# Two accumulation groups side by side in two PSUM banks, in a two-layer streaming encoder

## The chip, the cores and the metric

The kernel runs on one core of one Trainium2 chip. The metric is the device time of one execution in microseconds (us). Three executions of the kernel before took 1283.43, 1287.02 and 1288.18 us; the median is 1287.02.

Engines are named as the profile names them: PE is TensorE (matmuls), PEld its loading of weights, DVE is VectorE, ACT is ScalarE, POOL is GpSimd, SP is SyncE, which here issues the DMAs. PSUM, into which matmuls accumulate, has eight banks of 512 float32 columns in each of 128 partitions.

## The reference

The input x is (1, 512, 1024) float32. There are two layers. The first mixes by stick-breaking attention, the second by forgetting attention; both end with a gated feed-forward layer. Norms before and after each part are left out here.

```python
# layer 0: 16 heads of 64
q, k, v = split(a @ sb_w_qkv, 3)
h = h + rmsnorm(stick_breaking(q, k, v) @ sb_w_o)
# layer 1: softmax over s <= t of q.k/8 + fcum[t] - fcum[s]
kvf = rmsnorm(h) @ w_kvf            # keys, values, 16 forget gates
q = rmsnorm(h) @ fox_w_q
h = h + rmsnorm(forgetting(q, k, v, fcum) @ fox_w_o)
# at the end of each layer, d_ff = 2816
hdn = causal_conv_width_3(rmsnorm(h) @ w_up) + conv_b
gate, up = split(hdn, 2)
h = h + rmsnorm((gelu(gate) * up) @ w_down)
```

## The kernel before

**Matmuls in three passes.** Each float32 operand is kept as two exact parts, a high and a low one, and each product is made of three matmuls: high by high, high by low, low by high. The normalized activations are held feature-major as AH and AL, eight slices of 128 features by 512 tokens. A product over 1024 features is thus a group of 24 matmuls that accumulate into one PSUM region.

**Weights.** A stream of tiles of 512 KB is loaded in a fixed order by SP into two raw buffers. `make` (L127) splits each into its two parts, in ScalarE (L142, or L136 with a gain) and VectorE (L146, or L137). A ring of NW = 8 pairs of buffers holds them. `take` (L157) hands out the next tile and asks for the one eight places further on, which reuses the buffers of the tile handed out.

**Products with the weights stationary.** `w_stationary` (L205) runs the 24 matmuls (L211) of one group into one bank, 512 tokens wide, or 256 when it is called by halves. The feed-forward layer calls it through `up` (L574) for the gate and then for the up part of one chunk of 128 features, into the two banks of a pair; four pairs take turns over the 22 chunks. `gate` (L578) then applies the convolution (L585, L587), the GELU (L592) and the product (L593). The first three chunks (EARLY) are run by halves of the tokens, since the later token blocks come later. `gates` (L291) uses the function for the forget gates.

**Projections of the attention.** `project` (L345 and on) makes the query and the key of one pair of heads: it takes the query's tile, runs its group into one bank and reads this out (L357 and, in layer 1, L359 on ScalarE, L360 on VectorE, for each half of the partitions); then it takes the key's tile, runs its group into the other bank and reads that out (L369, L370 on ScalarE, L371 on VectorE). `project_v` makes the values of two pairs of heads: for each of the four token blocks it runs 24 matmuls of 256 columns (L389), two blocks to a bank, and reads a bank out (L394, L395). Both functions get their banks from `bank("pj")`, banks 4 and 5 in turn, except at the start of an attention, where banks that are not yet otherwise in use are passed in.

**Heads.** `head` (L400 and on) makes one head's scores (L409) in banks 0 to 2, its weights on ScalarE and VectorE, transposes them on TensorE (L456) into banks 6 and 7 and multiplies them with the values (L468) in bank 3.

**Order.** `run` writes, for each pair p: head (p, 0), the projection of pair p + 1, head (p, 1) and, for every second pair, the values of the next two. The framework's scheduler lays down each engine's order when the program is built, from this order of writing and from when it expects an instruction's inputs and buffers; semaphores are set by it, in PSUM by bank. So matmuls of a projection and of heads stand mixed on TensorE.

**Token-major products.** `unit` (L504) does the two products that follow, with the activations stationary and two banks in turn (L511). In the last block of the last layer `down_proj` runs it for one bank at a time.

Of the kernel before, what the change touches and what calls it, by code (L numbers as in the profile page):

```python
# [14 lines left out]
P = 128  # L15
T = 512
D = 1024
# [15 lines left out]
# Column offset of each query block's row of scores, and its width.  # L33
# [9 lines left out]
def tile_trunk(  # L43
# [29 lines left out]
    # All of PSUM, by banks. Attention: scores 0-2, weighted values 3, projections 4-5, transposes 6-7.  # L73
    # Elsewhere: pairs of banks, one for each token block or chunk of features in flight.
# [15 lines left out]
    # mask_a keeps keys before the query, mask_b those up to it.  # L90
# [10 lines left out]
    # Residual stream by token blocks; normalized activations, feature-major, in two parts.  # L101
# [9 lines left out]
    # Row p stands for head p % 16 and is of kind p % 64 // 16: kinds 0, 2 or 3, 1; less 2, 0 or 1, less 3.  # L111
# [3 lines left out]
    # ---- weight stream: each tile arrives whole and is split into two exact parts. Pool takes few of them:  # L115
    # it and DVE's operations on two operands in SBUF exclude each other. ----
# [88 lines left out]
    def w_stationary(ps, w, t0=0, t1=T, m=P):  # L205
        hi, lo = w
        n = 3 * KT
        i = 0
        for k in range(KT):
            for a, b in ((hi, AH), (hi, AL), (lo, AH)):  # L210
                nc.tensor.matmul(ps, a[:, k, :m], b[:, k, t0:t1], start=i == 0, stop=i == n - 1)  # L211
                i += 1

# [1 line left out]
    def rstd_of(ss):  # L215
        """(sum / D + eps) ** -0.5 of ss's first column, into its column 3."""
        nc.gpsimd.tensor_scalar(ss[:, 2:3], ss[:, 0:1], 1.0 / D, EPS, op0=ALU.mult, op1=ALU.add)  # L217
        nc.gpsimd.tensor_tensor(out=ss[:, 3:4], in0=ss[:, 2:3], in1=mhalf, op=ALU.pow)
        return ss[:, 3:4]

    def pre_block(b, g, t4, junk):
        """Normalizes block b of the residual and puts it into AH and AL."""
# [14 lines left out]
    def post_block(b, y, g, t4, junk):  # L237
        """Adds the normalized y to block b of the residual."""
        ss = small.tile([P, 4], F32, name="ss")
        nc.scalar.activation(junk, y, AF.Square, accum_out=ss[:, 0:1])  # L240
        nc.vector.tensor_tensor(out=t4, in0=y, in1=g, op=ALU.mult)
        r = rstd_of(ss)
        nc.vector.scalar_tensor_tensor(
            out=H[:, b, :], in0=t4, scalar=r, in1=H[:, b, :], op0=ALU.mult, op1=ALU.add
        )

    def finish(b, y, g, t4, junk):
        """post_block for the last block, by halves, with its way out."""
# [22 lines left out]
    class Attn:  # L271
# [19 lines left out]
        def gates(self):  # L291
            """Running sums of the log forget gates, and what adds fcum[t] - fcum[s] to a head's scores:
            rows (fcum in two parts, 1, 1) by query times rows (1, 1, -fcum in two parts) by key, the rows
            of all heads, 16 to a kind, in both halves of the partitions."""
# [14 lines left out]
            for t0 in (0, T // 2):  # L309
                w_stationary(ps[:, t0 : t0 + T // 2], ws, t0, t0 + T // 2)  # L310
# [27 lines left out]
        def gate_keys(self, p):  # L338
            """The rows by key of pair p's heads."""
# [5 lines left out]
        def project(self, p, halves=1, banks=None):  # L345
# [4 lines left out]
            w = take()  # L350
            ps = PS[:, banks[0], :] if banks else bank("pj")
            n = T // halves
            for j in range(halves):
                w_stationary(ps[:, j * n : (j + 1) * n], w, j * n, (j + 1) * n)
# [9 lines left out]
            w = take()  # L364
            ps = PS[:, banks[1], :] if banks else bank("pj")
            for j in range(halves):
                w_stationary(ps[:, j * n : (j + 1) * n], w, j * n, (j + 1) * n)
# [8 lines left out]
        def project_v(self, g, banks=None):  # L376
# [3 lines left out]
            for b0 in range(0, NB, per):  # L380
                ps = PS[:, banks[b0], :256] if banks else bank("pj")
                for b in range(b0, b0 + per):
                    sl = slice(b * P, (b + 1) * P)
                    o = slice((b - b0) * 256, (b - b0 + 1) * 256)
                    i = 0
                    for k in range(KT):
                        hi, lo = (w0, w1)[k // 4]
                        for a, m in ((AH, hi), (AH, lo), (AL, hi)):
                            nc.tensor.matmul(ps[:, o], a[:, k, sl], m[:, k % 4, :], start=i == 0, stop=i == 3 * KT - 1)  # L389
                            i += 1  # L390
# [9 lines left out]
        def head(self, p, hh):  # L400
# [38 lines left out]
            else:  # L439
                # exp(z), guarded where sigmoid(z) is 1 and its complement under float32's rounding.  # L440
# [79 lines left out]
    def out_proj(done, heads_end):  # L520
        """Block by block, around the last head's transposes and products."""
# [38 lines left out]
    def ffn_phase(l, heads_end, post_g, next_g, final):  # L560
        with tc.tile_pool(name=f"ffn{l}", bufs=2) as pool:
# [12 lines left out]
            def up(c, w, t0, t1):  # L574
                for i in range(2):
                    w_stationary(pair_of(c)[:, i, t0:t1], w[i], t0, t1)
# [132 lines left out]
```

## Time and profile before

| what | value |
|---|---|
| runs | 1283.43, 1287.02, 1288.18 us |
| profiled execution, span from the first to the last instruction | 1282.6 us; no other time of it is shown |
| instructions | 16820 |
| PE busy | 1241.5 us (97%) in 6485 matmuls |
| PEld busy | 1054.6 us (82%) |
| DVE busy | 811.0 us (63%) |
| ACT busy | 644.4 us (50%) |
| POOL busy | 101.8 us (8%) |
| DMA | 111.97 MB, 87 GB/s |
| mean granted TensorE clock | 0.996 of full speed |

The busy time of PE counts each matmul to its modelled end, and successive matmuls overlap, so the pace of matmuls is to be read from their starts or from their number in a stretch. The heads of the first attention run until about 247 us, its product with the output weights and the feed-forward layer until about 648 us, the second attention until about 850 us, and the rest is the second feed-forward layer. In a timeline the columns are start, duration, engine, line, operation, output and inputs, shape and count; in square brackets stands how long the engine was idle before, and what ended that. In the chain a row is start, duration and what the time was spent on.

### The profile page before, as it was taken

To read this page: it belongs to the slowest core of one execution; us is meant where nothing else is said; L and a number is where in the kernel's file an instruction comes from. 1 tells how busy PE (TensorE), PEld (TensorE's weight loads), DVE (VectorE), ACT (ScalarE), POOL (GpSimd) and SP (SyncE) were. 2 spreads that over 40 slices of the span, in tenths; PEclk is the share of its full clock that TensorE was granted. 3 is DMA by queue.
4 is the path that set the end of the run, shared out by engine and by line. 5 is a ranking of instruction groups with operands and counts; after the bars stand their busy time and mean duration, and the time that the engine had idled before them with its cause. 6 is when DMAs were issued, how large, how long until landed. Compare 5 with 4: busy or idle time off the path is not lost.

```text
span 1282.6 us, 16820 instructions
## 1 busy us (share of the span) xinstructions
PE 1241.5 (97%) x6485; PEld 1054.6 (82%) x6485; DVE 811.0 (63%) x1304; ACT 644.4 (50%) x1085; POOL 101.8 (8%) x163
## 2 busy tenths in 40 slices
PE   6999998999999999999989999999999999999998
PEld 6888886789888888888888988978988888888886
DVE  6898899576655555433478887874685555554323
ACT  5767677454433333322488786674453333333221
POOL 1000003020000000000011212342100000000001
PEclk9999999999999999999999999999999999999999
DMA  6421212124333333333223122110543233323311
GB/s 214 138 66 50 67 50 66 33 86 144 101 97 99 92 90 99 88 109 90 75 68 99 51 82 67 50 51 33 148 132 98 84 97 99 94 87 98 99 33 66
DMA packets 145928, 111.97 MB, mean 87 GB/s; under 512 B 4680, under 2 KB 136120, under 8 KB 145848
## 3 DMA queue, kind: packets, MB, share of 16 engines
q1 hardware_dynamic: 145848, 110.90, 28.8%
q8 instruction: 51, 0.84, 0.3%
q14 instruction: 29, 0.24, 0.1%
HBM read 108.79 MB, written 2.10 MB: 86 GB/s over the span
## 4 chain that ended last, share of the span: by engine, by line
PE 77%; DVE 10%; ACT 5%; DMA 4%; issue 2%; POOL 0%; SPq 0%; DVEq 0%; POOLq 0%; ACTq 0%
PE PS L211 45%; PE PS L511 21%; PE PS L389 4%; PE PS L468 2%; PE PS L409 2%; DVE wlo L146 2%; DMA raw<-sb_w_qkv_dram 2%; DVE ec L446 2%; PE PS L456 2%; DMA raw<-w_up_dram 2%; DVE ec L448 1%; DVE PL L463 1%; ACT whi L142 1%; ACT whi L136 1%; ACT ec L445 1%
## 5 line engine op out<-in xcount | busy, mean ns | idle before, releaser
L211 PE MATMUL PS<-AH,whi 128*128 128x512 f32 (+1 forms) x1088 | 402.0, 370 | 5.5 <-DVE QS L360 3.8
L211 PE MATMUL PS<-AL,whi 128*128 128x512 f32 (+1 forms) x1088 | 401.2, 369 | 0.0
L211 PE MATMUL PS<-AH,wlo 128*128 128x512 f32 (+1 forms) x1088 | 401.0, 369 | 0.0
L146 DVE TENSOR_TENSOR wlo<-raw,whi 128x512 fp32r<-128x512 f32 x332 | 217.4, 697 | 224.5 <-ACT whi L142 223.7
L142 ACT CAST whi<-raw 128x1024 fp32r<-128x1024 f32 x172 | 180.4, 1049 | 237.9 <-PE PS L211 186.4
L211 PEld LDWEIGHTS PS<-AH,whi 128*128 128x128 f32 x1088 | 204.8, 188 | 43.5 <-DVE QS L360 4.9
L211 PEld LDWEIGHTS PS<-AH,wlo 128*128 128x128 f32 x1088 | 204.5, 188 | 36.7
L211 PEld LDWEIGHTS PS<-AL,whi 128*128 128x128 f32 x1088 | 204.8, 188 | 36.2
L587 DVE SCALAR_TENSOR_TENSOR hc<-PS,cw,hc 128x511 f32<-128x511 f32 (+1 forms) x176 | 130.7, 746 | 2.7
L511 PE MATMUL PS<-whi,al 128*128 128x512 f32 x352 | 109.5, 389 | 0.0
L511 PE MATMUL PS<-whi,ah 128*128 128x512 f32 x352 | 109.3, 389 | 0.0
L511 PE MATMUL PS<-wlo,ah 128*128 128x512 f32 x352 | 109.3, 389 | 0.0
L610 DVE TENSOR_TENSOR al<-act,ah 128x512 fp32r<-128x512 f32 x44 | 30.4, 690 | 117.4 <-ACT ah L609 117.4
L609 ACT CAST ah<-act 128x512 fp32r<-128x512 f32 x44 | 27.4, 622 | 144.7 <-PE PS L511 138.5
L217 POOL TENSOR_SCALAR ss<-ss 128x1 f32<-128x1 f32 x31 | 11.7, 376 | 830.9 <-ACT junk L240 764.8
L389 PE MATMUL PS<-whi,AH 128*128 128x256 f32 x256 | 74.1, 289 | 3.5 <-DVE AL L235 1.4
L511 PEld LDWEIGHTS PS<-whi,ah 128*128 128x128 f32 x352 | 66.1, 188 | 13.7
L511 PEld LDWEIGHTS PS<-whi,al 128*128 128x128 f32 x352 | 66.1, 188 | 13.7
L511 PEld LDWEIGHTS PS<-wlo,ah 128*128 128x128 f32 x352 | 66.1, 188 | 13.7
L389 PE MATMUL PS<-wlo,AH 128*128 128x256 f32 x256 | 74.0, 289 | 0.0
L389 PE MATMUL PS<-whi,AL 128*128 128x256 f32 x256 | 73.5, 287 | 0.0
L592 ACT ACTIVATE hc<-hc 128x512 f32<-128x512 f32 x44 | 27.8, 631 | 86.3 <-DVE hc L587 86.3
(130 smaller groups left out, 1758.9 us busy)
## 6 DMA issues: line engine op xcount, KB each, us to landing
raw<-w_up_dram SPq DMA_DIRECT2D x88, 512.0 KB
raw<-w_down_dram SPq DMA_DIRECT2D x44, 512.0 KB
raw<-sb_w_qkv_dram SPq DMA_DIRECT2D x24, 512.0 KB
raw<-w_kvf_dram SPq DMA_DIRECT2D x16, 512.0 KB
raw<-sb_w_o_dram SPq DMA_DIRECT2D x8, 512.0 KB
raw<-fox_w_q_dram SPq DMA_DIRECT2D x8, 512.0 KB
raw<-fox_w_o_dram SPq DMA_DIRECT2D x8, 512.0 KB
H<-x_dram SPq DMA_DIRECT2D x4, 512.0 KB
```

Source lines behind the costliest of these rows:

```text
L142: nc.scalar.copy(hi, raw)
L146: eng.tensor_tensor(out=fl[:, s], in0=fr[:, s], in1=fh[:, s], op=ALU.subtract)
L211: nc.tensor.matmul(ps, a[:, k, :m], b[:, k, t0:t1], start=i == 0, stop=i == n - 1)
L389: nc.tensor.matmul(ps[:, o], a[:, k, sl], m[:, k % 4, :], start=i == 0, stop=i == 3 * KT - 1)
L409: nc.tensor.matmul(z[:, ZOFF[b] : ZOFF[b] + n], a[:, b * P : (b + 1) * P], m[:, :n], start=i == 0, stop=i == len(passes) - 1,)
L446: nc.vector.tensor_tensor_scan(C[:, ::-1], self.R[:, ::-1], C[:, ::-1], 0.0, ALU.mult, ALU.add)
L456: tr = nc.tensor.transpose(zt[:, o : o + P], E[:, ZOFF[b] + j * P : ZOFF[b] + (j + 1) * P], ident)
L511: mm = nc.tensor.matmul(y[:, c, :], s[:, sl], m[:, 0, c * 512 : (c + 1) * 512], start=k == 0 and i == 0, stop=k == n - 1 and i == 2,)
L587: nc.vector.scalar_tensor_tensor(out=hc[:, s:], in0=y[:, i, : T - s], scalar=col[:, 2 - s : 3 - s], in1=hc[:, s:], op0=ALU.mult, op1=ALU.add,)
L592: uses_table(nc.scalar.activation(hs[0], hs[0], AF.Gelu_apprx_tanh))
L609: nc.scalar.copy(ah, act[:, k, :])
L610: nc.vector.tensor_tensor(out=al, in0=act[:, k, :], in1=f32(ah), op=ALU.subtract)
```

## The change

`w_stationary` gets lists: several outputs and as many weight tiles. For each slice and each pass it runs one matmul for each of them before it goes on, so that two groups of 24 become one sequence of 48 that alternates between two banks. `up` passes gate and up of a chunk together. `project` takes both tiles first, runs query and key together, then reads out the query's bank and after it the key's. `project_v`, where it uses banks 4 and 5, takes both banks first and runs blocks 0 and 2 side by side, then blocks 1 and 3, and reads both banks out after that; with four banks passed in it runs block after block as before and reads them all out afterwards. `gates` passes lists of one.

```diff
-    def w_stationary(ps, w, t0=0, t1=T, m=P):
-        hi, lo = w
+    def w_stationary(outs, ws, t0=0, t1=T, m=P):
         n = 3 * KT
         i = 0
         for k in range(KT):
-            for a, b in ((hi, AH), (hi, AL), (lo, AH)):
-                nc.tensor.matmul(ps, a[:, k, :m], b[:, k, t0:t1], start=i == 0, stop=i == n - 1)
+            for a, b in ((0, AH), (0, AL), (1, AH)):
+                for ps, w in zip(outs, ws):
+                    nc.tensor.matmul(ps, w[a][:, k, :m], b[:, k, t0:t1], start=i == 0, stop=i == n - 1)
                 i += 1
...
-            w = take()
-            ps = PS[:, banks[0], :] if banks else bank("pj")
+            ws = [take(), take()]
+            pq, pk = (PS[:, b, :] for b in banks) if banks else (bank("pj"), bank("pj"))
             n = T // halves
             for j in range(halves):
-                w_stationary(ps[:, j * n : (j + 1) * n], w, j * n, (j + 1) * n)
+                w_stationary([x[:, j * n : (j + 1) * n] for x in (pq, pk)], ws, j * n, (j + 1) * n)
+            ps = pq
...
-            w = take()
-            ps = PS[:, banks[1], :] if banks else bank("pj")
-            for j in range(halves):
-                w_stationary(ps[:, j * n : (j + 1) * n], w, j * n, (j + 1) * n)
+            ps = pk
...
-            for b0 in range(0, NB, per):
-                ps = PS[:, banks[b0], :256] if banks else bank("pj")
-                for b in range(b0, b0 + per):
-                    sl = slice(b * P, (b + 1) * P)
-                    o = slice((b - b0) * 256, (b - b0 + 1) * 256)
-                    i = 0
-                    for k in range(KT):
-                        hi, lo = (w0, w1)[k // 4]
-                        for a, m in ((AH, hi), (AH, lo), (AL, hi)):
-                            nc.tensor.matmul(ps[:, o], a[:, k, sl], m[:, k % 4, :], start=i == 0, stop=i == 3 * KT - 1)
-                            i += 1
+            if banks:
+                pss = {b: PS[:, banks[b], :256] for b in range(NB)}
+                groups = [(b,) for b in range(NB)]
+            else:
+                pss = {0: bank("pj"), 2: bank("pj")}
+                groups = [(0, 2), (1, 3)]
+            for grp in groups:
+                i = 0
+                for k in range(KT):
+                    hi, lo = (w0, w1)[k // 4]
+                    for a, m in ((AH, hi), (AH, lo), (AL, hi)):
+                        for b in grp:
+                            b0 = b // per * per
+                            nc.tensor.matmul(
+                                pss[b0][:, (b - b0) * 256 : (b - b0 + 1) * 256],
+                                a[:, k, b * P : (b + 1) * P], m[:, k % 4, :], start=i == 0, stop=i == 3 * KT - 1,
+                            )
+                        i += 1
+            for b0, ps in pss.items():
                 pv = ps.rearrange("p (b j h d) -> p j b h d", b=per, j=2, d=HD)
...
             def up(c, w, t0, t1):
-                for i in range(2):
-                    w_stationary(pair_of(c)[:, i, t0:t1], w[i], t0, t1)
+                w_stationary([pair_of(c)[:, i, t0:t1] for i in range(2)], w, t0, t1)
```

## Rows read from the trace of the kernel before

**Rows 1.** The chain that ended last, shares of the span by engine and line.
```profile
by line: PE PS L211 45.2%; PE PS L511 21.1%; PE PS L389 4.5%; issue 2.3%; PE PS L468 2.2%; PE PS L409 2.0%; DVE wlo L146 1.8%; DMA raw<-sb_w_qkv_dram 1.7%; DVE ec L446 1.6%; PE PS L456 1.6%; DMA raw<-w_up_dram 1.5%; DVE ec L448 0.9%; DVE PL
```

**Rows 2.** Stretches: length, busy PE, PEld, DVE, ACT, POOL (count), clock, DMA share, GB/s.
```profile
52.00:206.00 154.00, 146.80 (x881) 129.34 (x880) 143.22 (x180) 113.90 (x154) 5.53 (x4) 0.99 0.21 64
672.00:850.00 178.00, 174.82 (x1080) 155.20 (x1079) 146.10 (x326) 139.95 (x356) 47.80 (x65) 1.00 0.23 69
340.00:520.00 180.00, 180.00 (x773) 145.00 (x773) 98.26 (x147) 65.38 (x80) 0.00 (x0) 1.00 0.32 94
```

**Rows 3.** A stretch of a down-projection, L511 alone: PE and PEld.
```profile
530.00:640.00 110.00, 110.00 (x487) 91.10 (x486) 1.00 0.30 91
```

**Rows 4.** Timeline of TensorE, last product's end: start, us, engine, line, operation.
```profile
1270.85 0.39 PE L511 MATMUL PS<-whi,ah 128*128 128x512 f32 x1
...
1276.07 0.39 PE L511 MATMUL PS<-whi,al 128*128 128x512 f32 x1
```

**Rows 5.** Timeline of TensorE, a head's first scores.
```profile
56.51 0.39 PE L409 MATMUL PS<-KH,QS 128*128 128x512 f32 x1
56.74 0.39 PE L409 MATMUL PS<-KL,QS 128*128 128x512 f32 x1
56.97 0.34 PE L409 MATMUL PS<-KH,QS 128*128 128x384 f32 x1
```

**Rows 6.** The chain in the first attention, 110 to 130 us: start, us, what.
```profile
109.33 0.70 DVE QS L360
...
110.08 5.86 PE PS L211 x24
115.95 0.52 PE PS L409 x3
...
118.11 5.61 PE PS L211 x24
123.72 0.88 PE PS L409 x5
...
126.45 1.88 PE PS L389 x16
```

**Rows 7.** Timelines of ScalarE and VectorE, 116.5 to 123 us.
```profile
116.83 0.60 ACT L357 ACTIVATE QS<-PS 64x512 fp32r<-64x512 f32 x1
...
121.86 0.69 DVE L360 SCALAR_TENSOR_TENSOR QS<-PS,QS 64x512 fp32r<-64x512 f32 x1
```

**Rows 8.** The chain in the second attention, 738 to 763 us.
```profile
753.50 0.52 PE PS L409 x4
...
755.19 5.60 PE PS L211 x24
760.79 0.70 PE PS L409 x4
...
762.70 0.41 PE PS L389 x3
```

**Rows 9.** Timeline of VectorE, 760.5 to 761 us.
```profile
760.70 0.69 DVE L360 SCALAR_TENSOR_TENSOR QS<-PS,QS 64x512 fp32r<-64x512 f32 x1
```

**Rows 10.** What TensorE waited for: us in total, times, longest.
```profile
PE PS L211 <- DVE QS L360: 3.8, 3, 1.9
```

**Rows 11.** Weight splits: the group of L146 (us, mean ns); ScalarE's timeline.
```profile
L146 DVE TENSOR_TENSOR wlo<-raw,whi 128x512 fp32r<-128x512 f32 x332 | 217.4, 697 | 224.5 <-ACT whi L142 223.7
...
645.60 4.79 ACT L136 ACTIVATE whi<-raw,gcol 128x128 fp32r<-128x128 f32 x16
```

**Rows 12.** Stretches, columns as in the first table of stretches.
```profile
659.00:662.00 3.00, 1.36 (x13) 1.15 (x11) 1.74 (x6) 2.95 (x6) 0.74 (x2) 1.00 0.81 204
...
663.60:665.60 2.00, 2.00 (x12) 2.00 (x12) 0.82 (x1) 1.35 (x3) 0.00 (x0) 0.52 0.34 32
```

**Rows 13.** The chain, 640 to 700 us.
```profile
663.69 4.36 PE PS L389 x24
...
668.99 2.83 PE PS L389 x24
```

More of the change, by code (lines that the diff above doesn't have):

```diff
@@ L309, in gates @@
             for t0 in (0, T // 2):
-                w_stationary(ps[:, t0 : t0 + T // 2], ws, t0, t0 + T // 2)
+                w_stationary([ps[:, t0 : t0 + T // 2]], [ws], t0, t0 + T // 2)
             e = pool.tile([P, T], F32, name="ge", tag="ot", bufs=2)
```

## The prediction

> **What bounds the kernel now.** I read the chain of the work that ended last first. L211, the line the change touches most, is 45.2% of it, and L511, the token-major product, 21.1%; both are matmuls [rows 1]. So TensorE's own pace sets most of the time. The stages differ, though, and the table by stretches shows how. In the feed-forward stretch TensorE is busy throughout, and VectorE for 98.26 of 180 us. In the first attention VectorE is busy 143.22 of 154 us. In the second, VectorE is busy 146.10 and ScalarE 139.95 of 178 us, beside a TensorE at 174.82 [rows 2]. A slower turn there on any of the three engines shows up in the end.
>
> Next I read the pace of single matmuls, because the change alternates PSUM banks. In the middle of the up-projection, where TensorE runs L211 alone, 773 matmuls of 512 columns start in 180.00 us, 233 ns from start to start, all 24 of a group into one bank [rows 2]. L511 writes two banks in turn and starts 487 in 110.00 us, or 226 ns [rows 3]. That 7 ns is all that the trace offers to a theory of "the same bank twice costs time". Two other places speak against the theory. At the end of the last product the columns are done one bank at a time: 12 matmuls into one bank, then 12 into the next. Its 24 starts run from 1270.85 to 1276.07 us, 227 ns each, no slower than the alternating ones [rows 4]. And in a head's scores (L409) the first two 512-column matmuls write one bank and the third another: the starts are 56.51, 56.74 and 56.97, so the change of bank gains nothing [rows 5]. So the 7 ns go with L511's operands rather than with its banks.
>
> **The change, part by part.** The number of matmuls, their shapes, their operands and the weights loaded for each are unchanged. What moves is their order, and with it the time at which a PSUM bank is finished.
>
> *Gate and up (L576).* Per layer there are 19 chunks of 48 matmuls of 512 columns, and three chunks in halves. I cost the new order at nothing, by rows 4 and 5. The lower bound is L511's pace: 232.9 − 225.9 is 7.0 ns, times 2 x 912 matmuls, or −13 us. No steady stretch that I found has a slower pace for this shape, so the upper bound is 0. The gate's chain now starts one group of 24 later. Four pairs of banks take turns, so three further chunks (some 33 us) pass before a chunk's banks are wanted again. In the 11.2 us of a chunk VectorE works 6.1 us and ScalarE 4.1 us, weight splits and all [rows 2], so a chain of at most 10 us ends long before that. At the last chunk the down-projection's matmuls on earlier chunks cover it; without that cover the later start would cost up to half of it, 5 us a layer. Two weight tiles are now released together instead of one after the other. The ring holds eight, so the next load has three chunks of cover, with the DMA share at 0.32 [rows 2]: nothing.
>
> *Query and key (`project`).* This is where I expect the price. During the heads all projections use two banks, 4 and 5. Today a query group of 24 matmuls fills one; while the key group fills the other, the query's bank is read out by two L357 and two L360. That reading is slow, because it stands in the queues of ScalarE and VectorE behind the split of the next weight tile and the heads' work. In the first attention the query group from 110.08 ends at 115.95 [rows 6]. ScalarE reaches its first L357 at 116.83; the second L360 starts at 121.86 and takes 0.69 us [rows 7]. From the last matmul to the free bank that is 6.6 us. In the second attention a query group ends at 753.50 [rows 8] and its second L360 at 761.39 [rows 9]: 7.9 us. Today this lies beside the 5.6 us of the key's group and some 2 us of head matmuls on either side of it [rows 6, 8]. The cover just holds, and not always: the query group at 110.08 itself starts as an L360 ends [rows 6], and TensorE waits for L360 before L211 three times, 3.8 us in all [rows 10].
>
> After the change query and key end together. Both banks are then full, and no other projection may write either; only the heads' matmuls are left to TensorE. The reading also starts later. Both tiles are now taken before the read-out, so two tiles are split ahead of it in program order: one more is 1.4 us on VectorE in the first attention (two L146 of 697 ns), and 2.4 us on ScalarE in the second (half of 16 L136 in 4.79 us) [rows 11]. That gives about 8.0 and 10.3 us from the last matmul to the first free bank. The heads' matmuls that stand around a pair of groups today come to 2.2 + 2.7 = 4.9 us in the first attention [rows 6] and 1.7 + 1.9 = 3.6 us in the second [rows 8]. The upper bound of the exposed time is therefore 3.1 and 6.7 us for each of the seven projections, in all 7 x 9.8 = 69 us. The lower bound is nothing: a read-out that nothing delays (two L357 of 0.60 us and two L360 of 0.69 us in a row, 2.6 us [rows 7]) fits behind the heads' matmuls. Between these ends I take 2 us in the first attention, since part of the waiting is paid already [rows 10], and 4 us in the second, where TensorE now hardly waits and both other engines are about 80% busy [rows 2]. That makes 7 x 2 + 7 x 4 = 42 us. L511's pace is a lower bound here too: 2 x 7 x 48 matmuls at −7.0 ns, −5 us.
>
> The Trainium skill (PSUM — Partial Sum Buffer, "Summary: rules for kernel authors") says that PSUM is to be read from a bank other than the one matmuls write, and guarded by bank. By that rule a bank being read out is shut to TensorE for the whole read-out, and interleaving two groups shuts two banks at once. The trace agrees: the query group at 110.08 starts as an L360 ends.
>
> *Two blocks' values (L389).* The four blocks go in two interleaved pairs over the same two banks, three times a layer. Both banks again end together. No row here shows this read-out; its bank needs two pairs of instructions like the query's, so 2.6 us if nothing delays it, and the 2.7 us of head matmuls [rows 6] would cover that: nothing, with the seven projections' average price of 3 us each as upper bound, 18 us in all.
>
> *The start of each attention.* The first pair is projected in halves into banks of its own and now wants both weight tiles. The second is one split behind the first, 1.4 or 2.4 us [rows 11], which is the upper bound. I take nothing, since the values' matmuls can fill it.
>
> *Sum.* The profiled execution has a span of 1282.6 us; nothing else of its own time is shown. It lies 4.4 us under the median of the runs, 1287.0. The terms are 0 + 42 + 0 + 0, so the span would be 1324.6 us and the time 1329 us.
>
> **The rivals.** *The alternation pays (faster).* If L211 takes L511's pace once it alternates, 13 and 5 us are gained, and if the heads also cover the read-outs the time is 1287 − 18 = 1269 us. For it: 233 against 226 ns [rows 2, 3]. Against it: rows 4 and 5, and the waits that exist already. It decides as soon as less than about 11 us of the read-outs is exposed. Chance 0.15. With the gain and with the exposed read-outs the time is 1329 − 18 = 1311 us; chance 0.08.
>
> *Nothing happens.* The order on each engine is laid down when the program is built, and it may place scores and transposes into every window; TensorE then only changes the order of the same work, and the time is 1287 to 1293 us. For it: heads' matmuls stand between all groups already [rows 6, 8]. Against it: they are too few for windows of 8 us. Chance 0.17.
>
> *The clock falls in the new windows.* Between 659 and 662 us TensorE is busy for 1.36 of 3.00 us; the granted clock is 1.00 there and then 0.52, that is mostly the lower of its two levels, 1.2 GHz [rows 12]. A block of 24 L389 takes 4.36 us there against 2.83 us afterwards [rows 13], so a fall costs about 1.5 us. If each of the 20 turns of the two layers brought one, that is 30 us on top: 1359 us. For it: windows of several microseconds without other work. Against it: in the attention stretches the clock is 0.99 and 1.00 although TensorE waits there too [rows 2]. Chance 0.13. The Trainium skill (TensorE: Matmul & The Clock Gate, "A second HAM failure mode: psum-queue depth-cycling") describes such a kernel, which cycles through PSUM banks, idles briefly between groups and so loses its clock. By that rule this rival would come true; a clock of 0.99 in the first attention bears it out only faintly.
>
> **How the numbers follow.** The forecast, read-outs exposed at the old pace, has a chance of 0.47, and 1302 to 1347 us as its own range. With the rivals at 0.15, 0.08, 0.17 and 0.13 this makes 0.15 for faster, 0.17 for no change and 0.68 for slower. The bound of 0.5%, 6.4 us, is about what the runs' own spread lets one tell (1283.4 to 1288.2). The range takes in half of the fastest rival and the middle of the clock's: 1276 to 1360 us. It is wide because the exposed read-out has bounds of 0 and 69 us.
>
> **What would show it.** Right: L211 at 233 ns in the middle of the up-projections; new rows of TensorE waiting for L360, L371 and L395, several microseconds each, in the attentions alone, which get longer by some 14 and 28 us; feed-forward stretches as before. Wrong: a pace near 226 ns there, or attentions of the old length because the groups slide apart again, one bank running ahead of the other. The step most likely to fail is the size of the exposed read-out: it hangs on how the built order mixes the heads' work with the two full banks.

## The result

The changed kernel takes 1357.2 us (median of four runs, 1355.7 to 1364.8) against 1285.9 us for the kernel before on the same chip: a ratio of 1.057, 95% interval 1.054 to 1.060. That is 71 us slower, where 42 were forecast. The profiled execution is the longest of the four, with a span of 1363.1 us, so its stages overstate the loss by some 8 us.

The feed-forward stretches stayed as they were. Here is, from the chain of the kernel before, each layer's run of the up-projection (start, us, what, matmuls), and then the same rows of the changed kernel:

```profile
291.94 236.36 PE PS L211 x1112
921.27 235.48 PE PS L211 x1112
```

```profile
303.97 237.08 PE PS L213 x1112
...
999.77 237.43 PE PS L213 x1112
```

L213 is the old L211. The runs last as long as before, to within 2 us. From the start to the first run it is 12.0 us more. From the first run to the second, which takes in the second attention, it was 629.3 us and is 695.8, or 66.5 us more.

The stretches of the changed kernel that answer to [rows 2] (length, busy PE, PEld, DVE, ACT, POOL with counts, granted clock, DMA share, GB/s):

```profile
52.00:206.00 154.00, 138.33 (x817) 120.54 (x816) 133.25 (x169) 105.73 (x141) 2.55 (x2) 0.97 0.19 58
350.00:520.00 170.00, 170.00 (x730) 136.97 (x729) 88.23 (x137) 61.69 (x78) 0.00 (x0) 1.00 0.33 93
700.00:800.00 100.00, 78.22 (x388) 66.04 (x387) 63.56 (x159) 62.67 (x174) 15.19 (x26) 0.85 0.19 53
```

The middle row gives the pace: 170.00 us for 730 matmuls is 232.9 ns, as before, although each now follows one into another bank. The last row is the second attention. TensorE is busy for 78 of 100 us there and its mean granted clock is 0.85, where [rows 2] showed 174.82 of 178 us and 1.00. VectorE and ScalarE are busy for less of the time as well, 64 and 63 of 100 us: no engine is full, and all wait for each other.

What TensorE waited for (us in total, times, longest), to be held against [rows 10]:

```profile
PE PS L417 <- ACT ec L437: 17.8, 7, 6.6
PE PS L234 <- DVE t L231: 14.3, 4, 8.1
PE PS L476 <- DVE PL L471: 11.6, 5, 4.4
PE PS L476 <- ACT PH L470: 10.9, 7, 4.5
PE PS L464 <- DVE PL L471: 5.7, 4, 2.6
```

L234 belongs to the norms and waited before too, 12.1 us. The others are matmuls of heads: scores (L417), transposes (L464) and weighted values (L476). The waits of projections for a bank to be read out remained short: L213 for L363, L403 and L371 comes to 5.2 us in all. The prediction had looked for the loss in rows of that kind. The heads' matmuls stand in front of the next group in TensorE's order, so the waits are booked to them.

One window shows how the two belong together. This is the changed kernel's chain around the end of a query-and-key group; in the matching place before [rows 8] it ran on TensorE alone:

```profile
780.12 2.34 PE PS L213 x10
...
782.49 2.45 ACT whi L136 x8
784.94 0.48 ACT QS L360
785.42 0.48 ACT QJ L362
785.90 0.58 ACT whi L136 x2
786.48 0.47 ACT KH L369
...
786.96 0.58 ACT KH L370
...
787.87 1.26 ACT whi L136 x4
789.13 0.25 ACT PH L470
789.39 0.30 ACT whi L136
789.69 1.68 ACT ec L437 x6
...
791.39 0.59 ACT QS L360
791.99 0.49 ACT QJ L362
...
792.50 0.70 DVE QS L363
...
793.25 0.79 PE PS L213
```

ScalarE's own timeline adds what it waited for before the first of these, and TensorE's what held it up meanwhile:

```profile
782.49 2.45 ACT L136 ACTIVATE whi<-raw,gcol 128x128 fp32r<-128x128 f32 x8 [1.63 <-PE PS L213]
```

```profile
782.52 0.63 PE L213 MATMUL PS<-AH,wlo 128*128 128x512 f32 x2
...
789.44 0.58 PE L476 MATMUL PS<-PH,V 128*128 128x256 f32 x1 [4.50 <-ACT PH L470]
790.41 0.79 PE L417 MATMUL PS<-KH,QS 128*128 128x512 f32 x1 [0.39 <-ACT ec L437]
...
793.25 0.79 PE L213 MATMUL PS<-AH,whi 128*128 128x512 f32 x1 [0.98 <-DVE QS L363]
793.84 0.63 PE L213 MATMUL PS<-AL,whi 128*128 128x512 f32 x1
794.27 0.63 PE L213 MATMUL PS<-AH,wlo 128*128 128x512 f32 x1
794.70 0.63 PE L213 MATMUL PS<-AH,whi 128*128 128x512 f32 x1
```

Read it from the top. At 782.46 the query's group is done with the high part of its weights; the last matmuls of both groups, the row of two at 782.52, end at 783.15. ScalarE has waited for the former, since the next two weight tiles are split into the buffers that query and key leave, and both leave them now. (A take fills the buffers of the tile taken just before it, one place nearer than the description ahead of the prediction puts it.) Two splits of eight L136 then stand in its queue among the read-outs. The copy that a head needs for its next product (L470) comes after most of them, at 789.1, so the head's matmuls, which were to cover the window, are themselves held up. The next group starts at 793.25, 10.1 us after the end of the last.

This window is one of the longer ones. In the second attention six query-and-key turns end with both banks full. From the last matmul to the next group's first it takes 10.7, 9.6, 10.1, 7.6, 7.4 and 7.7 us there, and each time the next group starts 0.05 to 0.07 us after the query's second L363 has ended. So it is the bank's read-out that lets the next group go, whatever line the waits are booked to. Heads' matmuls keep TensorE busy for 2.9 to 4.5 us of each window.

The clock pays as well. Two stretches of the changed kernel, columns as above, answer to [rows 12]:

```profile
784.80:789.40 4.60, 0.14 (x2) 0.00 (x0) 4.54 (x14) 4.56 (x14) 0.00 (x0) 0.93 0.28 76
789.40:796.50 7.10, 5.69 (x14) 4.23 (x15) 4.66 (x13) 5.14 (x14) 1.79 (x3) 0.50 0.32 101
```

After 4.6 us with next to no work, the granted clock is 0.50, the lower level of 1.2 GHz. The starts at 793.84, 794.27 and 794.70 are 0.43 us apart instead of 0.23.

### The profile page after: what moved, and what is told of

It is laid out like the page before. It is cut to its first block, busy times and chain, and to the rows that moved or that the text cites. A ratio compares the mean times of both kernels' runs of the same rounds, so it can differ in the third digit from the quotient of the medians.

```text
span 1363.1 us, 16852 instructions
## 1 busy us (share of the span) xinstructions
PE 1275.9 (94%) x6485; PEld 1079.2 (79%) x6485; DVE 797.8 (59%) x1304; ACT 641.5 (47%) x1085; POOL 101.3 (7%) x163
## 3 DMA queue, kind: packets, MB, share of 16 engines
q1 hardware_dynamic: 145848, 110.90, 27.5%
## 4 chain that ended last, share of the span: by engine, by line
PE 65%; ACT 5%; DVE 5%; DMA 2%; issue 1%; POOL 0%; DVEq 0%; POOLq 0%; ACTq 0%; SPq 0%
PE PS L213 41%; PE PS L519 18%; PE PS L393 3%; ACT whi L136 2%; DMA raw<-w_up_dram 2%; PE PS L476 1%; PE PS L464 1%; PE PS L417 1%; DVE wlo L146 1%; DVE wlo L137 1%; ACT ec L437 1%; DVE st L436 1%; DVE t L231 0%; ACT junk L226 0%; DVE QS L363 0%
## 5 line engine op out<-in xcount | busy, mean ns | idle before, releaser
L146 DVE TENSOR_TENSOR wlo<-raw,whi 128x512 fp32r<-128x512 f32 x332 | 213.8, 695 | 257.4 <-ACT whi L142 257.3
L213 PE MATMUL PS<-AH,whi 128*128 128x512 f32 (+1 forms) x1088 | 336.8, 376 | 5.2 <-DVE QS L363 2.2
L213 PE MATMUL PS<-AL,whi 128*128 128x512 f32 (+1 forms) x1088 | 334.1, 374 | 0.0
L213 PE MATMUL PS<-AH,wlo 128*128 128x512 f32 (+1 forms) x1088 | 333.1, 373 | 0.0
L213 PEld LDWEIGHTS PS<-AH,whi 128*128 128x128 f32 x1088 | 199.9, 192 | 44.7 <-DVE QS L363 3.1
L213 PEld LDWEIGHTS PS<-AH,wlo 128*128 128x128 f32 x1088 | 199.8, 192 | 38.0
L213 PEld LDWEIGHTS PS<-AL,whi 128*128 128x128 f32 x1088 | 200.1, 192 | 37.1
L594 DVE SCALAR_TENSOR_TENSOR hc<-PS,cw,hc 128x510 f32<-128x510 f32 (+1 forms) x176 | 120.0, 739 | 0.0
L470 ACT CAST PH<-PS 128x512 fp32r<-128x512 f32 (+1 forms) x96 | 47.5, 516 | 66.6 <-PE PS L464 56.0
L471 DVE TENSOR_TENSOR PL<-PS,PH 128x512 fp32r<-128x512 f32 (+1 forms) x96 | 55.5, 594 | 30.8 <-ACT PH L470 30.1
L393 PE MATMUL PS<-wlo,AH 128*128 128x256 f32 x256 | 69.0, 295 | 0.0
```

Source lines behind the costliest of these rows:

```text
L146: eng.tensor_tensor(out=fl[:, s], in0=fr[:, s], in1=fh[:, s], op=ALU.subtract)
L213: nc.tensor.matmul(ps, w[a][:, k, :m], b[:, k, t0:t1], start=i == 0, stop=i == n - 1)
L393: nc.tensor.matmul(pss[b0][:, (b - b0) * 256 : (b - b0 + 1) * 256], a[:, k, b * P : (b + 1) * P], m[:, k % 4, :], start=i == 0, stop=i == ...
L470: nc.scalar.copy(PH[:, :o], zt[:, :o])
L471: nc.vector.tensor_tensor(out=PL[:, :o], in0=zt[:, :o], in1=f32(PH[:, :o]), op=ALU.subtract)
L594: nc.vector.scalar_tensor_tensor(out=hc[:, s:], in0=y[:, i, : T - s], scalar=col[:, 2 - s : 3 - s], in1=hc[:, s:], op0=ALU.mult, op1=ALU.add,)
```

## The experiments

Ratios are to the kernel before, measured beside each run. The first table splits the profiled span. "First part" is from the start to the first up-run; "second part" is from the first up-run to the second. "Idle" and "slow" are worked out from TensorE's timeline in the second attention and what follows it up to the second up-run: each distance between two starts less the steady pace of that shape (233 ns for 512 columns, 118 for 256); an excess above 0.3 us counts as idle, a smaller one as slow pace. All entries are differences in us to the kernel before, whose values stand in the first row.

| kernel | first part | second part | of it idle | of it slow |
|---|---|---|---|---|
| before | 291.9 | 629.3 | 10.7 | 12.8 |
| changed | +12.0 | +66.5 | +50.1 | +14.8 |
| query and key alone | +10.7 | +19.1 | +17.0 | +2.3 |
| values alone | +1.0 | +21.1 | +14.0 | +6.7 |
| half lag | +4.8 | +9.4 | +7.9 | +1.5 |
| splits tied behind read-outs | +15.3 | +16.5 | +13.3 | +3.1 |
| before, splits tied | +7.0 | +0.5 | +1.7 | -2.0 |
| half lag and splits tied | +9.0 | +6.7 | +6.2 | +0.9 |

A second table goes by the turns of the second attention. The scheduler lays down the order, and it did not always keep the alternation that was written. Where it did up to the end, TensorE's timeline shows rows of two like matmuls (x2), as at 782.52 above; where it did not, the query's read-out starts while the key's group still runs. An entry is TensorE's idle time between a query-and-key turn and the next group, in us, and how the turn's two groups end: "t" together, "a" a whole group of 24 matmuls apart, "h" 13 matmuls apart. The next work after turn 7 is no projection any more.

| kernel | 1 | 2 | 3 | 4 | 5 | 6 | 7 |
|---|---|---|---|---|---|---|---|
| before | 2.0 a | 0 a | 0 a | 0 a | 0 a | 0 a | 3.8 a |
| changed | 8.7 t | 5.9 t | 7.2 t | 4.2 t | 5.7 t | 4.2 t | 5.2 a |
| query and key alone | 8.7 t | 5.9 t | 0 a | 0 a | 0 a | 0 a | 7.9 t |
| half lag | 8.2 h | 0 h | 0 a | 0 a | 0 a | 0 a | 5.0 h |
| splits tied behind read-outs | 4.5 t | 3.7 t | 2.4 t | 0 a | 0.7 t | 0 a | 6.0 t |

In the changed kernel three value turns add 3.7, 5.1 and 1.2 us. In its first attention only four of the seven query-and-key turns end together.

**Gate and up alone.**

```diff
-                for i in range(2):
-                    w_stationary(pair_of(c)[:, i, t0:t1], w[i], t0, t1)
+                w_stationary([pair_of(c)[:, i, t0:t1] for i in range(2)], w, t0, t1)
```

> The kernel before, with the gate and up products alone interleaved; query, key and values as before. Theory (banks come free later in attention; the alternation itself is worth nothing): ratio 0.998 to 1.002, about 1286 us, and both up-run stretches of the chain within 2 us of before's 236.4 and 235.5 us. Rival (alternation changes the pace of matmuls everywhere): the 1088 matmuls of the two FFN phases each gain or lose up to 7 ns, 6 to 14 us either way, ratio 0.989 or 1.011.

Measured: 1284.5 us, ratio 0.999 (0.998 to 1.001). The two up-runs in its chain:

```profile
290.50 236.35 PE PS L211 x1112
...
920.55 235.49 PE PS L211 x1112
```

They last 236.35 and 235.49 us, as before to within 0.01 us, and here the built order does alternate throughout. Alternating banks changes no pace, and the rival falls.

**Query and key alone.** `project` as in the change, the rest as before.

> The kernel before, with query and key alone interleaved; gate, up and values as before. Theory: this is the whole of the loss but for a few us, because both projection banks are full at once and TensorE has nothing to write into while they are read out: ratio 1.045 to 1.057 (1344 to 1359 us), and most of it in layer 1, whose projection turns stand idle some 7 us each. Rival (query/key costs what the prediction gave it, 42 us, and the values the other 29 us): 1328 us, ratio 1.033.

Measured: 1314.6 us, ratio 1.023 (1.020 to 1.027), some 30 us. Neither number came: it is less than both. A stretch of its second attention shows why (columns as above):

```profile
740.00:860.00 120.00, 120.00 (x754) 108.35 (x754) 92.07 (x215) 88.57 (x232) 28.14 (x43) 0.99 0.22 65
```

TensorE is busy for all of 120 us in the middle of the attention. The loss sits in turns 1, 2 and 7. In between nothing is lost because nothing is fused: in turns 3 to 6 the built order runs the two groups one after the other, as before. Turn 4 in the chain, query and then key, and the query's first read-out (L358) on ScalarE while the key's group runs:

```profile
774.62 5.60 PE PS L211 x24
...
782.13 5.66 PE PS L211 x24
```

```profile
782.28 0.58 ACT L358 ACTIVATE QS<-PS 64x512 fp32r<-64x512 f32 x1
```

**Values alone.** `project_v` as in the change, the rest as before.

> The kernel before, with the values of two blocks alone interleaved. Theory: the two value banks now also fill together and are read out together, 6 turns outside the start, so 0 to 18 us, about 8: ratio 1.000 to 1.014. Rival (the values carry what the prediction missed): about 29 us, ratio 1.022.

Measured: 1303.8 us, ratio 1.015 (1.012 to 1.018), some 19 us, just past the upper edge of the range. The first table puts all but 1 us of it into the second part. There TensorE idles 4.6 and 4.2 us after the first two value turns and not after the third; in the third, and in all three of the first attention, the built order runs the blocks one after the other. The two parts alone make 49 us and the whole change 71. The remaining 22 us are no cost of the combination as such: with both edits the built order ends turns 3 to 6 together as well, which it did not with query and key alone, and these four turns hold 21.3 us of idle time.

**A control for the pace: tiles moved by 32 bytes.** The kernel before, with one constant moved.

```diff
-    mhalf = const.tile([P, 1], F32, name="mhalf")
-    nc.vector.memset(mhalf, -0.5)
...
     kind = const.tile([P, 8], F32, name="kind")
+    mhalf = kind[:, 7:8]
+    nc.vector.memset(mhalf, -0.5)
```

> The kernel before with nothing interleaved; one 4-byte constant is moved into a spare column of another tile, so that every later tile of SBUF begins 32 bytes earlier, on a multiple of 64 bytes. It asks why 512-column matmuls run at 233 ns in the projections and the up-run but at 227 ns in the down-run, in both kernels. If the place of the moving operand in SBUF sets it: about 226 ns everywhere, 2 x 1088 + some 700 matmuls by 6.5 ns, 15 to 20 us less, ratio 0.985 to 0.988. If it does not: ratio 0.999 to 1.001 and 233 ns still.

Measured: 1284.3 us, ratio 1.000 (0.998 to 1.001). Its up-projection, at the place of the last of [rows 2], runs 773 matmuls in 180.00 us, 232.9 ns:

```profile
340.00:520.00 180.00, 180.00 (x773) 145.02 (x772) 98.29 (x146) 66.13 (x82) 0.00 (x0) 1.00 0.32 94
```

So a place 32 bytes further down does not remove the 7 ns. Other places were not tried.

**The splits written later, first one, then both.** In the changed kernel, `take` without its refill. In the first kernel the key's refill is written behind the query's read-out, still ahead of the key's; in the second all refills of query, key and values are written behind their read-outs. The first one's edit:

```diff
-            ws = [take(), take()]
+            ws = [take(), take(False)]
...
+            ahead(nused[0] - 1 + NW)
```

> The changed kernel, but the weight split that the key's tile sets off is put behind both read-outs instead of ahead of them. Theory (the split is half of what delays the read-out): 1.4 us per projection in the first attention and 2.4 us in the second come back, up to 7 x 3.8 = 27 us, 1331 to 1347 us, ratio to the kernel before 1.037 to 1.048. Rival (only the two full banks count, the splits fall into time that is lost anyway): 1354 to 1360 us, ratio 1.054 to 1.059.

> The changed kernel with all weight splits that query, key and values set off put behind their read-outs. Theory (what stands in ScalarE's queue ahead of the read-out sets the exposed time; the split in front waits for the very matmuls whose bank is to be read and then takes 2.4 us): two splits, 4.9 us, leave each of the ten windows of the second attention, and 2.8 us those of the first, as far as they are exposed: 25 to 45 us come back, 1312 to 1332 us, ratio 1.022 to 1.037. Rival (full banks alone): less than 10 us back, ratio above 1.048.

Measured: 1358.1 us, ratio 1.059 (1.056 to 1.061), and 1359.5 us, ratio 1.059 (1.057 to 1.062): nothing back. By the numbers the rival had won. But the splits had not moved. ScalarE's timeline of the second of these kernels (L364 is the first read-out of the query):

```profile
780.81 2.45 ACT L136 ACTIVATE whi<-raw,gcol 128x128 fp32r<-128x128 f32 x8 [3.51 <-PE PS L217]
783.17 0.57 ACT L364 ACTIVATE QS<-PS 64x512 fp32r<-64x512 f32 x1
```

The scheduler still put the split in front, and so it did in the first kernel. So these two runs say nothing for either theory; they say that the order of writing does not decide the order on the engine here.

**The splits tied behind the read-outs.** The same, but each refill is held behind the last read-out on ScalarE and on VectorE, in `project` and `project_v`:

```diff
+    def refill(*behind):
+        with ExitStack() as stack:
+            for i in behind:
+                stack.enter_context(tc.issue_after(ins(i)))
+            ahead(nused[0] - 1 + NW)
...
-            ws = [take(), take()]
+            ws = [take(False), take(False)]
...
+            refill(ia, iv)
```

> The changed kernel with the weight splits that query, key and values set off tied behind the last read-out of their own step on ScalarE and on VectorE (in the two kernels before, they were only written later, and the built order on ScalarE put them in front again). Theory (the clump on ScalarE between the groups' end and the head's own copy sets the idle time: two splits of 2.4 us, then the read-outs): 15 to 35 us come back, 1322 to 1342 us, ratio 1.030 to 1.045. Rival (full banks alone, or a head's chain that has no cover left): less than 8 us back, ratio above 1.050.

> The kernel before with the same splits tied behind the read-outs: the control for the run with tied splits. Theory (the other group covers the read-out already, only 3.8 us of waits for a query's bank are left): 0 to 4 us faster, ratio 0.996 to 1.001. Rival (the split is what makes the second attention tight even before): 8 us or more faster, ratio below 0.994.

Measured: 1321.2 us, ratio 1.028 (1.025 to 1.030); the control 1291.5 us, ratio 1.005 (1.003 to 1.007). Half of the loss is gone, a little more than the theory's range. ScalarE's timeline of the first kernel shows the new order in turn 3, whose groups still end together: the key's last two read-outs (L376, L377) and then both splits:

```profile
775.10 0.58 ACT L376 CAST KH<-PS 64x512 fp32r<-64x512 f32 x1
775.69 0.58 ACT L377 CAST KH<-PS 64x512 fp32r<-64x512 f32 x1
776.18 4.80 ACT L136 ACTIVATE whi<-raw,gcol 128x128 fp32r<-128x128 f32 x16
```

The window of this turn is 5.0 us long (770.22 to 775.22) instead of 10.1. In the second part the loss falls from 66.5 to 16.5 us, while the control moves by 0.5 there. Not all of that is the splits' doing, since the tied order also set turns 4 and 6 and the third value turn apart. In the turns that end together in both kernels (1, 2, 3 and 5) idle time falls from 27.5 to 11.3 us; after turns 4 and 6 it falls from 8.4 to 0. In the first part tying costs 7.0 us in the control, which I had not expected and have not traced.

**Half the overlap.** The changed kernel, but the second group of each fused pair starts half a group late:

```diff
-    def w_stationary(outs, ws, t0=0, t1=T, m=P):
+    def w_stationary(outs, ws, t0=0, t1=T, m=P, lag=0):
         n = 3 * KT
+        abc = [(k, a, b) for k in range(KT) for a, b in ((0, AH), (0, AL), (1, AH))]
+        for j in range(n + lag * (len(outs) - 1)):
+            for q, (ps, w) in enumerate(zip(outs, ws)):
+                i = j - lag * q
+                if 0 <= i < n:
+                    k, a, b = abc[i]
...
+                w_stationary([x[:, j * n : (j + 1) * n] for x in (pq, pk)], ws, j * n, (j + 1) * n, lag=0 if banks else 12)
...
+                order = list(mms(0)) + [x for ab in zip(mms(1), mms(2)) for x in ab] + list(mms(3))
```

> The changed kernel with half the overlap: the key's group begins 12 matmuls after the query's, and the second value bank 24 matmuls of 256 columns after the first, so that the first bank of each pair is finished 2.8 us before the second. Theory (both banks finished at once is the cause): up to 2.8 us of each of the 20 windows come back, 25 to 50 us, 1307 to 1332 us, ratio 1.018 to 1.037. Rival (the order of the groups' ends does not matter, only that the steps are fused into one block of 48): 1345 us or more, ratio above 1.046.

Measured: 1303.1 us, ratio 1.015 (1.012 to 1.017): 54 us back, more than the theory asked. A lag of 2.8 us gave back 57 us over the ten turns of the second part (66.5 - 9.4), or some 5 us a turn when the 8 us are taken off by which the changed kernel's profile is long. The surplus is there because the lag on the chip is not the one that was written. Turn 4, from the chain, and the query's first read-out on ScalarE (L358):

```profile
762.08 5.60 PE PS L213 x24
...
769.28 1.87 PE PS L213 x8
...
771.66 3.79 PE PS L213 x16
```

```profile
769.18 0.58 ACT L358 ACTIVATE QS<-PS 64x512 fp32r<-64x512 f32 x1
```

The query's bank is read from the 24th matmul on, while all 24 of the key's still follow. In turns 3 to 6, and in the first two value turns, the built order has undone the fusing altogether. Only turns 1, 2 and 7 have the lag as written, and after turn 1 it did not help (8.2 us against 8.7). So this run says what setting the groups apart gives back; what half a group does is seen in three turns alone, and the rival, that only the fusing matters, is not refuted by it. Shares by line from 700 to 800 us, for the kernel before, the changed kernel and the half lag:

```profile
by line: PE PS L211 48.3%; PE PS L389 23.0%; PE PS L409 10.5%; PE PS L468 9.8%; PE PS L456 8.7%
```

```profile
by line: PE PS L213 31.6%; ACT whi L136 12.8%; PE PS L393 9.1%; DVE wlo L137 6.1%; PE PS L417 5.7%; PE PS L476 4.2%; PE PS L464 3.6%; ACT ec L437 3.3%; ACT QS L360 3.2%; ACT QJ L362 2.9%; DVE st L436 2.9%; ACT KH L370 2.3%; issue 2.3%; DVE 
```

```profile
by line: PE PS L213 41.5%; PE PS L398 21.6%; PE PS L421 8.1%; PE PS L480 8.1%; PE PS L468 7.1%; DVE wlo L137 4.2%; ACT whi L136 2.3%; DVE st L440 1.5%; DVE QS L361 1.4%; DVE oT L490 0.7%; DVE KL L369 0.7%; issue 0.6%; ACT QS L358 0.6%; ACT 
```

Before, the chain in these 100 us is TensorE's alone. In the changed kernel weight splits (L136 and L137) are 19% of it. In the half-lagged kernel L136 falls from 12.8 to 2.3%: where the groups are apart, the query's bank is free earlier, its tile's buffers are too, and the split that goes into them runs beside the key's matmuls, as it did before.

**Half lag and tied splits.** Both edits, the tying in the second attention alone.

> The half-lagged kernel with the splits tied behind the read-outs as well, in the second attention alone (in the first, tied splits cost 7 us by their control). Theory (the exposed time of a window is what is left of one path: splits and read-outs, less what still covers them; without the splits 1.7 us a window were left, with the lag alone 0.9 us): both together leave nothing in the second attention, and 4.8 us of the first, 1286 to 1294 us, ratio 1.001 to 1.007. Rival (what is left with the lag, 9 us in the second attention, has another cause): 1299 us or more, ratio above 1.011.

Measured: 1298.7 us, ratio 1.011 (1.009 to 1.014). That is the rival's number, to a hair; the theory's is missed. The second part is still 6.7 us longer than before, although neither full banks nor splits should be left in it. The first part is 9.0 us longer against 4.8 with the lag alone, though the instructions of the first attention stand in the same order on TensorE, ScalarE and VectorE in both kernels. So 4 us is what two profiled executions can differ by, and the 6.7 us are not far above that. Their cause stays open. Here the built order does keep the lag as written, in turn 1 and in 3 to 7. Idle time after turn 1 falls from 8.2 to 1.9 us, and after turns 3 to 6 there is none, as the theory had it; what is left stands after turn 2 (2.7 us), the values (2.2 us) and the last turn (5.4 against 3.8 before).

**A third bank for the projections**, taken from the transposes, in the changed kernel and in the kernel before:

```diff
-        b = {"pj": 4, "zt": 6}[kind] + turn[kind] % 2
+        b = (4, 5, 7)[turn[kind] % 3] if kind == "pj" else 6
```

> The changed kernel, but the projections turn over three banks (4, 5, 7) and the transposes have bank 6 alone. To be read against the next kernel, which is the kernel before with the same banks. Theory (both banks full is the cause): TensorE can run ahead with one more group while two banks are read, so the loss against that control falls from 71 us to 10 to 35 us. Rival (the heads' own chain is late, because read-outs and splits of two tiles stand in a clump before its exponentials and copies): the loss against the control stays at 55 us or more.

> The kernel before with three banks for projections and one for transposes: the control for the kernel just above. Both theories: a head's three rounds of transposes now queue behind one bank, 16 heads a layer, so 0 to 40 us slower than before, ratio 1.00 to 1.03.

Measured: 1397.1 us, ratio 1.089 (1.086 to 1.091), and the control 1401.4 us, ratio 1.092 (1.089 to 1.095). The control was expected within 40 us and lost some 118. With one bank for transposes a head is so slow that fusing the groups costs nothing on top (1397 against 1401). This fits a third bank that helps and as well a loss that merely hides behind a longer wait, so it decides nothing.

## Why the prediction was right, and where it fell short

**Direction and place: right.** Slower, through banks that end together in the attentions; feed-forward stretches and pace unchanged. That gate and up cost nothing was right by the run with them alone. So the rivals "the alternation pays", "gain and loss" and "nothing happens" fell, the last not wholly: the built order set the groups apart again in four of the fourteen query-and-key turns, where the forecast had counted on all of them ending together. The sign that was named, waits of several microseconds for L360, L371 and L395, did not show either (5.2 us in all); the windows show in the waits of heads' matmuls.

**The window's length: right, towards its long end.** 10.3 us from the last matmul to the first free bank were worked out for the second attention, the additional split in ScalarE's queue included. The six turns that end together have 7.4 to 10.7 us, 8.8 in the mean.

**The exposed part of that window: somewhat more than taken.** The step is "between these ends I take 2 us in the first attention and 4 us in the second". For the first, 14 us were forecast; query and key alone measured 10.7 and the whole change 12.0. That this came so near is partly luck, since only four of the seven turns end together there. For the second, 28 us were forecast; the idle time after the seven turns is 35 us more than before, 5.6 us for each of the six that end together, under the bound of 6.7. The cover that the step took off, 3.6 us of heads' matmuls, was there (2.9 to 4.5 us), though late: their inputs come out of the same queues as the read-outs, and in the window above TensorE waited 4.50 us for L470 first.

**What was mis-sized: two terms that the sum put at nothing.** The second part grew by 66.5 us, and the 35 us explain about half. Idle time after value turns adds 10 us and slow pace 14.8; the rest, some 7 us, lies inside groups and behind the last turn, and the profiled execution is a long one.

**The values: a term of nothing that measured 19 us by itself.** The step supposed a read-out "if nothing delays it" of 2.6 us. In the second attention of the changed kernel it takes 6.7 us from the last matmul to the end of the last L403 in two of the three turns and 2.2 us in the third; in the first of them a split of 2.45 us stands among the read-outs in ScalarE's queue. The stated bound of 18 us was just passed by the values alone.

**The clock: a rival that came as an addition.** It was priced at 30 us on top of the forecast. Slow pace in the second part measures 14.8 us more than before, and it is smaller in every experiment with less idle time (3.1 us beside 13.3, 1.5 beside 7.9), though not in proportion (2.3 beside 17.0, 6.7 beside 14.0). That it follows from the windows is likely, but it was not tested by itself. The Trainium skill (TensorE: Matmul & The Clock Gate, "A second HAM failure mode: psum-queue depth-cycling") describes a kernel that cycles through PSUM banks, pauses between groups of matmuls and loses throughput to its clock; the trace agrees with it here, by the 0.50 after the pause.

**Cause, as far as shown.** Two edits that each leave the number and kind of instructions alone took back 36 us (splits tied behind the read-outs) and 54 us (groups apart). In both the built order also set turns apart by itself, so it is the turns, more than the totals, that tell the causes from each other. Where both groups end together, TensorE idles for 4.2 to 8.7 us, until the query's bank is read out. With the splits out of the way and the groups still ending together, idle time after the same four turns falls from 27.5 to 11.3 us. In turns 3 to 6, with the groups a whole group apart, there is none, whether the kernel is the one before, the one with query and key alone or the half-lagged one; and none with half lag and tied splits, where these groups are fused but end 13 matmuls apart. What is shown, then, is that ending both groups at once does the damage, more than half of it through the weight splits which that end releases. The Trainium skill (PSUM — Partial Sum Buffer, "Summary: rules for kernel authors") asks that PSUM be read from another bank than the one matmuls write; the turns kept apart, in which the query's bank is read while the key's is filled, agree by their idle time of 0. Whether more banks would do the same was not settled. No version beat the kernel before: gate and up alone equal it.

## What to carry to other kernels

Before two groups are fused so that they end together, list everything that their ends release, weight buffers as well as banks, and whose in-order queue all of that falls into at one moment. Work that is to cover the resulting window can come late if its own inputs come out of that queue. Read the built order of every version from its trace before its time is put down to an edit: here the scheduler left splits where they were, and it pulled apart groups that were written as one sequence. An order that matters on an engine has to be tied.

## What the runs showed of the hardware

One bank instead of two for a head's transposes cost some 118 us over 32 heads, with a third bank for the projections already in the balance; that is more than the change itself. A pause of 4.6 us was followed by 7.1 us at half the granted clock, matmuls 0.43 us apart. Why 512-column matmuls run at 232.9 ns in the projections and at 225.9 ns in the down-projection stays open: neither the bank sequence nor moving the tiles by 32 bytes changes it.
